# A hybrid pooling and recurrence block on one core: norm 2's reduction later, spare buffers elsewhere, and two results added in parts

## The chip, the cores and the metric

The kernel runs on 1 core of one Trainium2 chip. The metric is the device time of one execution in microseconds (us), lower is better. Time before: a median of 2389.03 us over 3 runs (2384.92 to 2390.30). The profiled execution is one more run of the same kernel; its own time was 2389.73 us, of which the profile covers a span of 2388.0 us.

The engines are TensorE (PE, matrix products; PEld is its weight loading), VectorE (DVE), ScalarE (ACT), GpSimd (POOL) and SyncE (SP). SP and POOL only issue transfers where nothing else is said. Each engine executes its instructions strictly in the order in which they stand in its program.

## The reference

One layer on 512 tokens of width 2048, with 16 learned tokens put in front:

```python
u = rmsnorm(h, norm1_g)
v_pool, v_lru, v_gelu, g_pool, g_lru = jnp.split(u @ w_in, IN_SPLITS, axis=-1)
pool_out = pool_mixer(v_pool, pool_w, pool_scale)  # 4 groups: mean of a causal window of
                                                   # 2, 4, 8, 16 tokens less the token, then a 512x512 map
xc = causal_depthwise_conv(v_lru, conv_w, conv_b)
r = sigmoid(xc @ gate_a_w + gate_a_b)              # 8 heads of 256
i = sigmoid(xc @ gate_x_w + gate_x_b)
a = exp(-8 * r * softplus(-lam))
lru = scan(h_t = a_t * h_(t-1) + sqrt(1 - a_t ** 2) * (i_t * xc_t)) * gelu(v_gelu)
merged = sigmoid(g_pool) * pool_out + sigmoid(g_lru) * lru
h = h + merged @ w_out
u2 = rmsnorm(h, norm2_g)                           # "norm 2"
h = h + square(relu(u2 @ mlp_w1)) @ mlp_w2         # 2048 -> 8192 -> 2048
out = rmsnorm(h, final_g)[:, 16:]
```

## The kernel before

**Products.** All products are in float32 precision. A weight w and an activation x are each split into a high part, which TensorE takes exactly, and the rest (whi and wlo, hi and lo), and each product is three matmuls: wh·xh, wh·xl, wl·xh (`mm3`, line 370). The big products (the two gates of the merge, the MLP up and down) are computed block by block by Strassen's method: a 2x2 block product takes seven products instead of eight, in the order x11, t1, t2, x21, t3, x22, t4, which are named after their activation operand (`strassen`, line 648). They collect in three PSUM banks A, B and C. A first takes x11; ScalarE copies it out as p1. B takes t1 (copied as q5). A goes on with t2 (copied as u2). C takes x21, A goes on with t3, B with x22, A with t4. VectorE and ScalarE put the four quadrants of the result together from banks and copies (`put("11")`, `"22"`, `"12"`, `"21"`). TensorE can only go on in a bank when the copy out of it is done: t2 waits for the copy p1, t3 for the copy u2, x22 for the copy q5, t4 for put 22.

**Weights.** Class `Weights` streams all weights in one fixed sequence. For each, a load is issued on SP (raw buffers; lines 107 and 111), VectorE forms sums of blocks where Strassen's method wants them (line 128), ScalarE makes the high part (line 137) and VectorE subtracts it to give the low part (line 138). There are 4 raw buffers, 4 pairs whi/wlo, 2 buffers of sums ("sum") and 2 that hold one block longer ("w21"). `advance()` puts the next set's work into the program at fixed points; `behind` and `hold` can order a set's sums or its copies behind a named instruction.

**Stages.** (1) The projections of the input. (2) A stretch in which the last head of the recurrence ("GA 7", gs70 and gs71 being its two blocks of 128 channels), the last pooling group ("VP 15", "PW 3") and the first gate product (`gl0`) meet. Here `evac_VP` takes channels 15 of the pooling out of PSUM (pv15), adds shifted copies of it four times on POOL (pw15, line 564; a window of 16 tokens), and forms pd15 on VectorE, whose two halves are TensorE's operand for the 48 matmuls of PW 3. ScalarE scales the results into po12 to po15 (line 586), which are stored to DRAM from SP; po buffers come in rotation, so that po14 takes one out of which an earlier store or load must have gone. `lru` runs the recurrence: two square roots (line 534, with a load of ScalarE's function table ahead of them), products, the scans on VectorE (line 545). (3) The 16 further gate products and the output projection. (4) Norm 2: its sum of squares, `ssq`, is collected on VectorE while the last part of h is formed; a matmul with a matrix of ones (`ps_r`, line 993, in `middle`) sums it over the 128 partitions, and a chain of six operations makes `rho` from it, by which the first MLP result, y0, is scaled. The first product of the MLP up runs with x11, x21 and t1 interleaved, since their last operands come late. (5) MLP up, 32 Strassen blocks. (6) MLP down: the blocks b1 to b38. The first two groups, [1, 3] and [2, 4], and [32, 38], [33, 37], [34, 36] near the end are computed in pairs by `strassen_pair` (line 725), which shares each weight between two blocks; in a pair, p1, u2 and q5 of the second block need a place of their own (`spare`): p1 and u2 lie in the tile `scale`, which is free by then, and q5 lies in the last quarter of the second block's result tile e (`es[1][:, 3 * HS :]`, HS is 256). The result e of a block up to b33 is added into h in DRAM by one accumulating transfer issued on POOL, `hsp<-e` (line 1115). e1 and e2, and e3 and e4, use the same two buffers by turns. Operands of later blocks are read from DRAM into slots (line 1028), split by ACT and DVE (lines 1044 and 1045).

The order on each engine is the program's order after a scheduler has moved instructions between the fixed points; the pieces quoted with the change are from that final order.

## Time and profile before

| | |
|---|---|
| median of 3 runs | 2389.03 us (2384.92 to 2390.30) |
| profiled execution, its own time | 2389.73 us |
| its span | 2388.0 us |
| mean granted TensorE clock | 0.994 |
| TensorE busy | 2347.3 us (98%), 40.7 us of the span without a matmul |
| weight loading (PEld) | 2300.1 us (96%) |
| VectorE | 1922.5 us (81%) |
| ScalarE | 1212.3 us (51%) |
| GpSimd | 315.5 us (13%) |
| data moved | 418.73 MB, 175 GB/s on average |

[...] A row of a timeline gives the start, the duration, the engine, the line of the kernel, the operation, out<-in with the names of the program (buffer numbers left out), partitions x elements, how many instructions the row holds, and in brackets how long the engine was idle just before and what ended that. A row of windows gives a stretch, its length, each engine's busy time in it with the number of instructions, the granted TensorE clock (1.00 is full speed), the share of the DMA engines and the GB/s they moved. Line numbers are those of the kernel before.

### The profile page before, as it was taken

What the parts mean: (1) busy time and instruction counts of PE and PEld (TensorE: products, weight loads), DVE (VectorE), ACT (ScalarE), POOL (GpSimd) and SP (SyncE); (2) the same over time, 40 slices, a digit from 0 to 9 for tenths busy, and PEclk for the clock granted to TensorE, in tenths of its full rate; (3) what the DMA queues carried; (4) which work ended last, traced back from release to release, by engine and by line L of the source; (5) the groups of instructions that cost most, each with busy time, mean ns of one, the idle gap of its engine ahead of it and who ended that gap; (6) DMA issues with size and microseconds to landing.
All of it is one profiled execution on the core that took longest, in us unless ns stands there. A gap on an engine that the chain in (4) does not pass through costs nothing. (4 is left out here: it accounts for less than half of the span.)

```text
span 2388.0 us, 46263 instructions
## 1 busy us (share of the span) xinstructions
PE 2347.3 (98%) x19254; PEld 2300.1 (96%) x19254; DVE 1922.5 (81%) x2356; ACT 1212.3 (51%) x1632; POOL 315.5 (13%) x435
## 2 busy tenths in 40 slices
PE   8999999999999999999999999999989999999997
PEld 8999999989999999888999999999989999999997
DVE  7866766588888887378989888888879888888877
ACT  6654645355555554244445444444455555555544
POOL 0224342300000001033000000000110000000013
PEclk9999999999999999999999999999999999999999
DMA  5255554654444447568544544555576666666662
GB/s 198 89 168 173 172 177 166 257 186 150 143 149 143 151 149 261 181 209 283 186 156 153 161 153 159 167 166 162 173 213 173 186 181 182 196 188 188 175 185 107
DMA packets 115858, 418.73 MB, mean 175 GB/s; under 512 B 14112, under 2 KB 18080, under 8 KB 113984
## 3 DMA queue, kind: packets, MB, share of 16 engines
q1 hardware_dynamic: 77040, 253.40, 32.9%
q0 software_dynamic: 38464, 162.29, 21.0%
q8 instruction: 150, 2.46, 0.4%
q14 instruction: 60, 0.49, 0.1%
q10 hardware_dynamic: 144, 0.10, 0.0%
HBM read 324.89 MB, written 90.31 MB: 174 GB/s over the span
## 5 line engine op out<-in xcount | busy, mean ns | idle before, releaser
L138 DVE TENSOR_TENSOR wlo<-raw,whi 128x1024 fp32r<-128x1024 f32 (+2 forms) x388 | 467.2, 1206 | 116.9 <-ACT whi L137 112.9
L137 ACT ACTIVATE whi<-raw 128x1024 fp32r<-128x1024 f32 (+2 forms) x388 | 398.9, 1034 | 318.0 <-issue 78.9
L137 ACT ACTIVATE whi<-sum 128x1024 fp32r<-128x1024 f32 (+3 forms) x267 | 279.0, 1045 | 454.2 <-DVE sum L128 234.8
L138 DVE TENSOR_TENSOR wlo<-sum,whi 128x1024 fp32r<-128x1024 f32 (+3 forms) x267 | 320.1, 1199 | 73.0 <-ACT whi L137 68.1
L370 PE MATMUL ps_A<-a,whi 128*128 128x256 f32 x2048 | 354.5, 277 | 0.0
L370 PE MATMUL ps_Ab<-a,whi 128*128 128x256 f32 x1728 | 308.8, 279 | 4.1 <-ACT u_b L746 2.1
L370 PEld LDWEIGHTS ps_A<-a,whi 128*128 128x128 f32 x2048 | 308.6, 188 | 0.7 <-issue 0.5
L370 PE MATMUL ps_A<-a,wlo 128*128 128x256 f32 x1024 | 282.9, 276 | 0.0
L370 PEld LDWEIGHTS ps_Ab<-a,whi 128*128 128x128 f32 x1728 | 263.9, 190 | 4.7 <-DVE a L1045 2.4
L370 PE MATMUL ps_Ab<-a,wlo 128*128 128x256 f32 x864 | 240.6, 279 | 0.0
L128 DVE TENSOR_TENSOR sum<-sum,raw 128x1024 f32<-128x1024 f32 (+4 forms) x178 | 213.7, 1201 | 5.5
L370 PEld LDWEIGHTS ps_A<-a,wlo 128*128 128x128 f32 x1024 | 192.3, 188 | 0.0
L370 PE MATMUL ps_B<-a,whi 128*128 128x256 f32 x1024 | 177.5, 276 | 0.0
L370 PEld LDWEIGHTS ps_Ab<-a,wlo 128*128 128x128 f32 x864 | 164.2, 190 | 0.0
L370 PE MATMUL ps_vl<-a,whi 128*128 128x272 f32 (+1 forms) x896 | 163.3, 285 | 0.0
L370 PE MATMUL ps_vp<-a,whi 128*128 128x256 f32 (+1 forms) x896 | 162.8, 284 | 0.0
L370 PE MATMUL ps_wo<-a,whi 128*128 128x512 f32 x512 | 158.0, 390 | 0.0
L370 PEld LDWEIGHTS ps_B<-a,whi 128*128 128x128 f32 x1024 | 154.2, 188 | 0.0
L370 PE MATMUL ps_Bb<-a,whi 128*128 128x256 f32 x864 | 152.5, 276 | 0.4 <-DVE a L1045 0.4
L370 PE MATMUL ps_B<-a,wlo 128*128 128x256 f32 x512 | 141.5, 276 | 0.0
L128 DVE TENSOR_TENSOR sum<-w,raw 128x1024 f32<-128x1024 f32 (+3 forms) x89 | 106.5, 1197 | 40.1 <-DMA raw<-w 39.7
L370 PEld LDWEIGHTS ps_vl<-a,whi 128*128 128x128 f32 x896 | 138.2, 189 | 0.3
(336 smaller groups left out, 5854.2 us busy)
## 6 DMA issues: line engine op xcount, KB each, us to landing
raw<-w SPq DMA_DIRECT2D x168, 512.0 KB, 4.3
raw<-w_in SPq DMA_DIRECT2D x135, 512.0 KB, 3.8
w<-w SPq DMA_DIRECT2D x56, 512.0 KB, 4.2
a<-ysp POOLq DMA_DIRECT2D x20, 896.0 KB, 6.1
hsp<-e POOLq DMA_DIRECT2D x33, 512.0 KB, 6.5
ysp<-t POOLq DMA_DIRECT2D x31, 512.0 KB, 4.9
w<-w_in SPq DMA_DIRECT2D x24, 512.0 KB, 3.9
ysp<-y POOLq DMA_DIRECT2D x31, 384.0 KB, 5.1
```

The costliest lines, as they stand in the source:

```text
L128: nc.vector.tensor_tensor(self.raw[o], self.raw[x], self.raw[y], op=ALU.add)
L137: nc.scalar.activation(hi[:, s], raw[:, s], AF.Copy)
L138: nc.vector.tensor_tensor(lo[:, s], raw[:, s], hi[:, s].bitcast(F32), op=ALU.subtract)
L370: PE.matmul(o, a, b, start=first and i == 0, stop=last and i == 2, skip_group_check=True)
```

## The change

It has seven parts.

1. In the last pooling channel (c == 15) the four window additions run on VectorE instead of POOL.
2. po14 and po15 no longer take two rotating buffers but the two halves of one buffer of the weight sums (tag "sum"). Both square roots of the last head, not only that of its first block, are now ordered behind the copy p1 of gl0.
3. `behind` holds back the sums of the sets from first_set + 6 on, no longer from + 2, until the last scan is done, and `hold` orders set first_set + 5 behind gl0's copy u2.
4. Norm 2's matmul with ones, `ps_r`, stands behind t3 and x22 of the first MLP product instead of ahead of its t2. The chain to rho and y0's scaling follow it; ssq and v2 live in a pool of their own (`rs`) until then. `finish_h` stores h by halves of the channels instead of halves of the tokens.
5. In all pairs, q5 of the second block lies in the first half of `scale` (p1's place, so it is copied after put 11) instead of the last quarter of e.
6. The quadrants lie in e in another order (n = 1 - a + 2b), so that 22's half and 12's neighbour each other; the tables of channels and weights on the host side and the output's assembly follow it.
7. For the pairs [1, 3] and [2, 4] each block's e is added into h in three transfers (512 columns after put 22, which covers 11 and 22; 256 after put 12; 256 after put 21) instead of one.

```diff
+                                    else tc.issue_after(W.u2.ins) if i == W.first_set + 5
...
                 root = S.activation(r, r, AF.Sqrt)
-                if hd == HEADS - 1 and co == 0:
-                    W.root = root
+                if hd == HEADS - 1:
+                    W.roots.append(root)
...
-                W.behind = lambda i: (tc.issue_after(scan.ins) if 1 < i - W.first_set < 21
+                W.behind = lambda i: (tc.issue_after(scan.ins) if 5 < i - W.first_set < 21
...
-                G.tensor_tensor(n[:, lo:T], s[:, lo:T], s[:, lo - win : T - win], op=ALU.add)
+                (V if c == KD - 1 else G).tensor_tensor(n[:, lo:T], s[:, lo:T], s[:, lo - win : T - win], op=ALU.add)
...
-                z = (keep if g == 3 else tmp)(f"po{c}")[:, :SEQ]
+                if c == 14:
+                    last_two = sums_pool.tile([P, SW], F32, tag="sum", name="po14", bufs=2)
+                if c < 14:
+                    z = (keep if g == 3 else tmp)(f"po{c}")[:, :SEQ]
+                else:
+                    z = last_two[:, m % 2 * SEQ : (m % 2 + 1) * SEQ]
...
                 if name == "gl0":
-                    tc.add_manual_dep(W.root.ins, done.ins.name,
+                    for root in W.roots:
+                        tc.add_manual_dep(root.ins, done.ins.name,
...
         product(B, "x22", False)
+        if norm is not None:
+            norm(done)
         put("12", B, u2)
...
-        spare = {"p1": scale[:, :HS], "u2": scale[:, HS:SEQ], "q5": es[1][:, 3 * HS :]}
+        spare = {"p1": scale[:, :HS], "u2": scale[:, HS:SEQ], "q5": scale[:, :HS]}
...
         product(C, "x21", True)
+        put("11", C, p1)
         copy(q5[1:], B[1:])
-        put("11", C, p1)
...
-            n = a + 2 * b if by_half else 2 * a + b
+            n = 1 - a + 2 * b if by_half else 2 * a + b
...
+    def norm2(done):
+        t = bank("r", "", SEQ)
+        with tc.issue_after(done.ins):
+            PE.matmul(t, ones, ssq, start=True, stop=True, skip_group_check=True)
+        a, b = ssq, v2
+        V.scalar_tensor_tensor(rho, t, EPS * D, v2, op0=ALU.add, op1=ALU.mult)
...
+        norm_stage.close()
+        scaled_later.pop()()
...
+            if (j, c) == (0, "22") and z is not None:
+                scaled_later.append(lambda: put(c, o, None))
+                return
...
+    def adding(e, p):
+        put = put_plain(e, True)
+
+        def put_and_add(c, x, z):
+            put(c, x, z)
+            at = {"22": slice(HS, 3 * HS), "12": slice(3 * HS, 4 * HS), "21": slice(0, HS)}.get(c)
+            if at:
+                nc.gpsimd.dma_start(h_sp[p][:, at], e[:, at], accum_op=ALU.add)
+        return put_and_add
...
+            puts = [adding(e, x % WIN) if n < 2 else put_plain(e, True) for e, x in zip(es, g)]
...
-        if t < JS + 2:
+        if n >= 2 and t < JS + 2:
             for x, e in zip(g, es):
                 nc.gpsimd.dma_start(h_sp[x % WIN], e, accum_op=ALU.add)
```

ScalarE where PW 3 ends and gl0 begins, from po14 to the copy u2 of gl0. In the names, `ps_pw14` is a bank of PW 3, `gs700` and `gs701` are the roots' operands (blocks 0 and 1 of the last head), the first `scale_80<-ps_Agl0` row is the copy p1, the second the copy u2, and whi83 to whi85 are the high parts of gl0's t2, x21 and a later weight set. Before:

```order
L586 ACTIVATE po14_5475<-ps_pw14_5462,par_71 128x512
L527 ACTIVATE e71_5507<-e71_5507 128x528
L137 ACTIVATE whi83_5499<-raw83_5424 128x1024
L586 ACTIVATE po15_5491<-ps_pw15_5478,par_71 128x512
L534 ACT_TABLE_LOAD
L534 ACTIVATE gs701_5374<-gs701_5374 128x528
L672 ACTIVATE scale_80<-ps_Agl0_5548 128x256
L534 ACTIVATE gs700_5359<-gs700_5359 128x528
L137 ACTIVATE whi84_5628<-w2181_5414 128x1024
L137 ACTIVATE whi85_5660<-sum80_5418 128x1024
L700 ACTIVATE scale_80<-ps_Agl0_5548 128x256
```

With the change:

```order
L594 ACTIVATE po14_5475<-ps_pw15_5478,par_71 128x512
L138 ACTIVATE whi83_5498<-raw83_5424 128x1024
L530 ACTIVATE e71_5506<-e71_5506 128x528
L138 ACTIVATE whi84_5627<-w2181_5414 128x1024
L681 ACTIVATE scale_80<-ps_Agl0_5547 128x256
L537 ACT_TABLE_LOAD
L537 ACTIVATE gs700_5359<-gs700_5359 128x528
L537 ACTIVATE gs701_5374<-gs701_5374 128x528
L710 ACTIVATE scale_80<-ps_Agl0_5547 128x256
L138 ACTIVATE whi85_5659<-sum80_5418 128x1024
```

The two roots and their table load stood ahead of the copies p1 (one of them) and u2; now both stand behind p1. whi85 stood ahead of the copy u2, and now stands behind it.

TensorE in the first MLP product, where the interleaved x11, x21 and t1 end (`ps_A0`, `ps_C0`, `ps_B0` with whi284, whi285, whi286) and t2 begins (whi287). Before:

```order
L370 MATMUL ps_A0_12353<-a2_899,wlo284_12310 128x256
L370 MATMUL ps_C0_12355<-a2_899,whi285_12340 128x256 x2
L370 MATMUL ps_C0_12355<-a2_899,wlo285_12341 128x256
L370 MATMUL ps_B0_12354<-a2_899,whi286_12349 128x256 x2
L370 MATMUL ps_B0_12354<-a2_899,wlo286_12350 128x256
L993 MATMUL ps_r_12531<-ssq2_11054,ones_72 128x512
L370 MATMUL ps_A0_12353<-a1_84,whi287_12464 128x256 x2
L370 MATMUL ps_A0_12353<-a1_84,wlo287_12465 128x256
```

With the change the same place reads on from t1 to t2, and the matmul `ps_r` stands between x22 (whi289) and t4 (whi290):

```order
L371 MATMUL ps_B0_12356<-a1_84,whi289_12503 128x256 x2
L371 MATMUL ps_B0_12356<-a1_84,wlo289_12504 128x256
L371 MATMUL ps_B0_12356<-a1_84,whi289_12503 128x256 x2
L371 MATMUL ps_B0_12356<-a1_84,wlo289_12504 128x256
L1013 MATMUL ps_r_12572<-ssq2_11056,ones_72 128x512
L371 MATMUL ps_A0_12355<-a1_84,whi290_12540 128x256 x2
L371 MATMUL ps_A0_12355<-a1_84,wlo290_12541 128x256
L371 MATMUL ps_A0_12355<-a1_84,whi290_12540 128x256 x2
```

`ps_r` was ahead of t2; now the rows of t2, t3 and x22 stand ahead of it.

ScalarE in the pair [2, 4], from the copies p1 and q5 to put 21 (`u2_b2` is u2 of block 2, the `scale_80<-ps_Ab4` row behind it u2 of block 4, `ps_Bb4` is the bank out of which q5 of block 4 is copied; a2 is the slot that is split). Before:

```order
L746 ACTIVATE q5_b2_20044<-ps_Bb2_20038 128x256
L137 ACTIVATE whi517_20066<-sum344_20025 128x768
L137 ACTIVATE whi518_20089<-raw347_19968 128x768
L137 ACTIVATE whi519_20118<-w21345_19799 128x768
L746 ACTIVATE e4_20035<-ps_Bb4_20039 128x256
L746 ACTIVATE u2_b2_20043<-ps_Ab2_20036 128x256
L746 ACTIVATE scale_80<-ps_Ab4_20037 128x256
L1044 ACTIVATE a2_899<-a2_899 128x1536
L1044 ACTIVATE a2_899<-a2_899 128x256
L137 ACTIVATE whi520_20146<-sum344_20025 128x768
L137 ACTIVATE whi521_20172<-raw346_19945 128x768
L137 ACTIVATE whi522_20200<-raw348_19989 128x640
```

With the change:

```order
L757 ACTIVATE q5_b2_20045<-ps_Bb2_20039 128x256
L138 ACTIVATE whi517_20067<-sum344_20028 128x768
L138 ACTIVATE whi518_20090<-raw347_19965 128x768
L138 ACTIVATE whi519_20119<-w21345_19796 128x768
L757 ACTIVATE u2_b2_20044<-ps_Ab2_20037 128x256
L757 ACTIVATE scale_80<-ps_Ab4_20038 128x256
L1062 ACTIVATE a2_899<-a2_899 128x1536
L1062 ACTIVATE a2_899<-a2_899 128x256
L138 ACTIVATE whi520_20147<-sum344_20028 128x768
L138 ACTIVATE whi521_20175<-raw346_19942 128x768
L138 ACTIVATE whi522_20205<-raw348_19988 128x640
L138 ACTIVATE whi523_20233<-sum348_20231 128x640
L757 ACTIVATE scale_80<-ps_Bb4_20040 128x256
```

The copy of q5 of block 4 stood ahead of both u2 copies and wrote into e4; now it stands behind them and four weight copies, and writes into `scale`.

POOL at the same two pairs, before:

```order
L1028 DMA a1_84<-ysp8_131 128x1792
L1115 DMA hsp1_116<-e1_19875 128x1024
L1115 DMA hsp3_118<-e3_19876 128x1024
L1115 DMA hsp2_117<-e2_20034 128x1024
L1115 DMA hsp4_119<-e4_20035 128x1024
L1115 DMA hsp5_120<-e5_20233 128x1024
```

With the change:

```order
L1131 DMA hsp3_118<-e3_19873 128x256
L1131 DMA hsp1_116<-e1_19872 128x256
L1131 DMA hsp3_118<-e3_19873 128x256
L1131 DMA hsp2_117<-e2_20035 128x512
L1131 DMA hsp4_119<-e4_20036 128x512
L1131 DMA hsp2_117<-e2_20035 128x256
L1131 DMA hsp4_119<-e4_20036 128x256
L1131 DMA hsp2_117<-e2_20035 128x256
L1131 DMA hsp4_119<-e4_20036 128x256
L1146 DMA hsp5_120<-e5_20238 128x1024
```

Where each block had one transfer of 1024 columns it has three, of 512, 256 and 256 (the first rows of e1 and e3 stand above these).

61 lines of the change are left out of this document (30 added, 31 removed).

## The prediction

> **What bounds the kernel now.** I read the page's busy times first, then the waits of TensorE, then windows around each place that the change touches, and last single rows of the timeline there.
>
> ```profile
> span 2388.0 us, 46263 instructions
> PE 2347.3 (98%) x19254; PEld 2300.1 (96%) x19254; DVE 1922.5 (81%) x2356; ACT 1212.3 (51%) x1632; POOL 315.5 (13%) x435
> ...
> PE ps_Ab L370 <- ACT u_b L746: 5.3, 2, 3.3
> PE ps_Ab L370 <- DVE e L783: 2.8, 1, 2.8
> PE ps_Agl L370 <- ACT scale L700: 2.5, 1, 2.5
> ...
> PE ps_r L993 <- DVE ssq L859: 1.8, 1, 1.8
> PE ps_Bgl L370 <- ACT po L586: 1.5, 1, 1.5
> PE ps_Agl L370 <- ACT scale L672: 1.3, 1, 1.3
> ```
>
> TensorE is busy for 98% of the span, and the change takes no matmul away. So only time in which TensorE stands still, or runs below full speed, can be won: 40.7 us of stalls (2388.0 less 2347.3) and the slow stretches behind some of them. The waits view (us in total, times, longest) names the targets: the copies u_b (5.3 in two places: the pair [2, 4] and a pair near the end) and put e (2.8), both in the pairs; the copies into scale and po around gl0 (2.5, 1.5, 1.3); ssq at norm 2 (1.8). That is 15.2 us, a third of it all.
>
> The second part of the price is the clock. Windows, one for each place (columns: stretch; its us; busy us and count of PE, PEld, DVE, ACT, POOL; granted clock; DMA share; GB/s):
>
> ```profile
> 464.93:477.46 12.53, 11.73 (x50) 8.94 (x49) 7.16 (x7) 9.80 (x14) 4.67 (x5) 1.00 1.04 419
> 477.46:505.78 28.32, 23.03 (x169) 22.14 (x168) 22.18 (x27) 13.21 (x18) 1.68 (x3) 0.88 0.75 262
> 494.20:500.80 6.60, 6.44 (x29) 6.14 (x30) 6.25 (x8) 2.91 (x5) 0.33 (x1) 0.51 0.93 339
> 1118.00:1150.00 32.00, 30.16 (x245) 28.97 (x244) 31.87 (x50) 16.77 (x27) 4.92 (x8) 1.00 0.71 232
> 1757.60:1768.00 10.40, 7.15 (x38) 7.08 (x38) 6.08 (x9) 5.44 (x9) 0.00 (x0) 0.67 0.22 79
> 1780.70:1788.00 7.30, 4.52 (x25) 4.42 (x25) 6.63 (x10) 1.23 (x2) 0.49 (x1) 0.77 0.17 68
> 2307.30:2314.00 6.70, 4.65 (x27) 4.60 (x27) 3.92 (x6) 2.87 (x6) 2.75 (x6) 0.75 1.02 394
> ...
> 1835.88 5.48 PE ps_Ab L370 x48
> ```
>
> The last row, from the chain of waits, is a stretch that runs undisturbed: 48 matmuls of 256 columns in 5.48 us, 0.114 each. Against it every window can be priced by its count. The clock is at 0.51, 0.67, 0.77 and 0.75 in the windows behind the waits of 2.5, 3.3, 2.8 and 2.1 (the second of the 5.3), and 1.00 around norm 2, where the wait is 1.8.
>
> **The change, stage by stage.**
>
> *Around gl0 (parts 1 to 3).* The 168 matmuls of gl0 need 168 × 0.114 = 19.2 us and took 28.32, so 9.1 us are there; PW 3 took 12.53 with 11.73 busy, another 0.8. The ceiling is 9.9. What held it:
>
> ```profile
> 459.26 0.71 DVE L558 TENSOR_TENSOR pv<-ps_vp,scale 128x528 f32<-128x528 f32 x1 [2.38 <-PE ps_vp L370]
> 465.02 1.30 POOL L564 TENSOR_TENSOR pw<-pw 128x513 f32<-128x513 f32 x1
> 466.36 0.69 DVE L567 SCALAR_TENSOR_TENSOR pd<-pw,pv 128x512 f32<-128x512 f32 x1 [6.39 <-POOL pw L564]
> 481.09 0.69 ACT L586 ACTIVATE po<-ps_pw,par 128x512 f32<-128x512 f32 x1 [2.34 <-DMA pl<-po]
> 483.86 1.28 ACT L534 ACT_TABLE_LOAD   x1
> 485.15 0.64 ACT L534 ACTIVATE gs<-gs 128x528 f32<-128x528 f32 x1
> 485.70 0.36 ACT L672 ACTIVATE scale<-ps_Agl 128x256 f32<-128x256 f32 x1
> 487.73 1.26 DVE L545 TENSOR_TENSOR_SCAN xc<-n,gs 128x528 f32<-128x528 f32 x1
> 489.50 1.22 DVE L128 TENSOR_TENSOR w<-w,raw 128x1024 f32<-128x1024 f32 x1
> 490.75 1.07 ACT L137 ACTIVATE whi<-w 128x1024 fp32r<-128x1024 f32 x1 [4.16 <-DVE w L128]
> 493.88 0.37 ACT L700 ACTIVATE scale<-ps_Agl 128x256 f32<-128x256 f32 x1
> ```
>
> VectorE waits 6.39 us for POOL's four additions. On VectorE they cost about what pv and pd do, 0.7 each: 459.97 + 4 × 0.7 = 462.8, so pd is ready near 463.5 instead of 467.05, before PW 3 starts at 464.93, and wins its 0.8. ScalarE then waited 2.34 for the transfer of an old po; a buffer of the sums is free by then, so the po copies follow the matmuls of PW 3. The table load (1.28) and a root (0.64) stood ahead of copy p1 and stand behind it now. The weight copy at 490.75 waited 4.16 for a sum that VectorE had put behind the scan, and the copy u2 (493.88) stood behind it; now that sum stands ahead of pv.
>
> The new chain, laid out with these durations: po15 at 476.8 to 477.5, the two weight copies to 479.7, p1 to 480.1, table and roots to 482.5; TensorE ends PW 3 near 476.2, x11 at 478.9, t1 at 481.6, t2 at 484.3, u2 is copied at once. ScalarE is ahead of TensorE throughout. Next to be late is VectorE: the scans move forward with the roots, to end near 487.3, and the low half of set first_set + 5, held behind u2, near 488.5, against x22's start at 489.8: 1.3 us of margin. VectorE's own new load is 2.8 us at a place where it idled 6.39. On SP, a load of weights moves ahead of stores of pooled results, and these ahead of stores of the scans; with a DMA share of 1.04 in PW 3 no queue there can be moved for free, but what reads these stores comes with the end of the gates' first blocks, 20 us on. Bounds: the whole 9.9; or half, 5, if VectorE's chain takes the place of ScalarE's, with a wait behind which the clock drops again. The margin of 1.3 is nearer the first: I take **9**.
>
> *Norm 2 (part 4).*
>
> ```profile
> 1128.43 1.23 DVE L138 TENSOR_TENSOR wlo<-sum,whi 128x1024 fp32r<-128x1024 f32 x1
> 1130.31 1.12 PE L993 MATMUL ps_r<-ssq,ones 128*128 128x512 f32 x2 [1.84 <-DVE ssq L859]
> 1133.04 1.22 DVE L138 TENSOR_TENSOR wlo<-sum,whi 128x1024 fp32r<-128x1024 f32 x1
> ```
>
> The 1.84 us on ssq go, but VectorE is busy for 31.87 of the 32 us of this window, and TensorE lives on what it makes. t2's low weights end at 1129.66; t2 (24 matmuls, 2.72) then ends near 1132.4 and x22's low weights are ready only at about 1134.0 (1134.26 before). So TensorE waits there instead, and ps_r is paid later (0.57, from its start to t2's at 1130.88, up to its 1.12). The chain to rho lies behind x22 and is needed only by y0, behind TensorE's work. Bounds: 0.7 won, if the rho chain's removal brings the low weights as much forward, or 1.5 lost, if both ps_r and a later y0 count in full. I take **0**.
>
> *The first two pairs (parts 5 to 7).*
>
> ```profile
> 1749.19 1.79 POOL L1115 DMA_DIRECT2D hsp<-e  x2 [6.77 <-ACT e L781]
> 1760.21 0.38 ACT L746 ACTIVATE e<-ps_Bb 128x256 f32<-128x256 f32 x1 [5.92 <-DMA hsp<-e]
> 1760.38 0.83 DVE L128 TENSOR_TENSOR sum<-w,raw 128x640 f32<-128x640 f32 x1 [3.51 <-DMA raw<-w]
> 1764.89 0.95 DVE L138 TENSOR_TENSOR wlo<-sum,whi 128x768 fp32r<-128x768 f32 x1
> 1770.64 0.39 ACT L781 ACTIVATE e<-ps_Ab 128x256 f32<-128x256 f32 x1 [0.97 <-PE ps_Ab L370]
> 1772.04 7.83 DMA raw<-w
> ...
> DMA to landing us min/median/max: 5.3/7.2/10.1
> ...
> DMA to landing us min/median/max: 7.2/8.6/10.1
> ```
>
> The last two lines are landing times of the accumulating transfers: of the eight between 1749 and 1841, and of the first two alone. q5 of block 4 waited 5.92 on ScalarE until e3's transfer, the second, had landed (1750.0 + 10.1 = 1760.1); the u2 copies behind it held t3. By count, 1757.6 to 1768.0 lost 10.40 − 38 × 0.114 = 6.1 us and 1780.7 to 1788.0 7.30 − 25 × 0.114 = 4.5: 10.6 in all. With q5 in scale, u2 is copied right behind t2, and t3's 18 matmuls run from 1757.6 to 1759.7. But the wait on e is not gone: put 11 of block 2 and then of block 4, on VectorE, write into the buffers that e1's and e3's transfers read, and now all three of each must have landed. Behind these puts are queued the sum of 1760.38, a slot's split and the low weights of x22 (1764.89 before). The parts are issued as the quadrants are ready, from 1746.8 on instead of 1749.19, but POOL spends about 0.9 us on each issue (1.79 for two): six take 5.1 us, the last goes out by about 1751.9, against 1750.98. The same bytes start 2.4 us earlier, so the load behind the 3.51 lands earlier as well. Laid out: low weights of x22 at 1761.5 to 1762.7 instead of 1764.89 + 0.95, a stall of some 2 us instead of 3.25, and the end of the block at 1766 to 1768 instead of 1770.64: 2.5 to 4.4 won. The load at 1772.04 took 7.83 because it ran beside the whole transfers of e2 and e4; now it goes out 3 to 4 us earlier, with half of those bytes gone before, and most of the second 4.5 is won. Bounds: 2 (the first dip stays) to 10.6 (both go). I take **7**, the middle of the first and nearly all of the second.
>
> *Near the end (part 5 alone).*
>
> ```profile
> 2308.69 0.38 ACT L746 ACTIVATE e<-ps_Bb 128x256 f32<-128x256 f32 x1 [5.74 <-DMA hsp<-e]
> 2318.74 0.63 ACT L1137 ACTIVATE a<-a 128x512 fp32r<-128x512 f32 x1 [3.73 <-DMA a<-ysp]
> ```
>
> The same q5 waited 5.74; the window lost 6.70 − 27 × 0.114 = 3.6. e's transfer is whole here as before, so only put 11 still waits until 2308.6, at VectorE. What is late next is the read of ysp that ended the wait of 3.73 at 2318.74, which does not move; up to 1 us is given back there, more if it reaches further (bound 1.5). I take **3**.
>
> The sum is 9 + 0 + 7 + 3 = 19: the profiled execution's 2389.73 becomes 2370.7. The median lies 0.70 below that execution: **2370.0**.
>
> **Rivals.**
>
> *The pairs keep their first dip* (the puts of e2 and e4 wait for the last part, issued 0.9 later than the whole one was). For it: that later issue and the median landing of 7.2. Against it: the bytes start earlier. The pairs then bring 2.5: 2374.5.
>
> *VectorE takes over around gl0*, and 5 are won of 9: 2374.0. For it: 22.18 of 28.32 us busy there. Against it: the margin of 1.3.
>
> *The clock does not depend on these stalls.* Then the slow stretches stay, losing 6.60 × 0.49 + 10.40 × 0.33 + 7.30 × 0.23 + 6.70 × 0.25 = 10.0 us, and only 9 of 19 come: 2380. Against it: each dip stands right behind a wait of about 2.0 us or more, and none behind 1.84. [...]
>
> *Slower: the parts are served one after the other, each at the price of a whole one.* At 5.3 each, six last 31.8 us, from 1746.8 to 1778.6; put 11 and what VectorE has behind it (0.83 + 2.1 + 0.42 + 0.95 = 4.3) would bring x22's low weights to 1782.9, 17 us later than before, and the second pair perhaps 8 more. Less the 12 won elsewhere: 2389.0 + 25 − 12 = 2402. It decides from about 4.2 us a part, where the pairs lose 12. Against it: a transfer's bytes are halved or quartered, and whole ones overlapped: the first two, issued 0.9 apart from 1749.2 on, landed after 7.2 and 10.1, the second 3.8 behind the first. [...]
>
> *Nothing happens*, because the load of 1760.38 or another transfer holds each place at the same time: 2389.
>
> **How the numbers follow.** Forecast 0.60; pairs keep the dip 0.15; VectorE takes over 0.12; clock 0.05; nothing 0.03; slower 0.05. The low end takes the winning bounds: 9.9 + 0.7 + 10.6 + 3.6 = 24.8, so 2364.2. The high end takes the losing ones, 5 − 1.5 + 2 + 1.5 = 7, so 2382; a little inside it, at 2381, all cases but the last two are held. A measurement of this kernel can tell about 0.2% (4.8 us) from no change; all cases but the last two win more: faster 0.92, same 0.03, slower 0.05.
>
> **What the profile after would show.** Right: pd follows pv without a wait on POOL; no waits of TensorE on po or scale around gl0, and the clock at 1.00 there; gl0's window near 20 us. At norm 2 ps_r without a wait on ssq, but a wait of the same size on a low weight or a copy. In the pairs, no ScalarE wait on hsp<-e ahead of u2; the next wait of x22 below 2.5 us. Wrong: VectorE waiting for hsp<-e at put 11 past 1762; landings of the parts above 4.2 us one after another; a dip of the clock where no stall stands; new waits in gates' first blocks for the stores of the scans.

## The result, and the profile after

The changed kernel takes 2371.59 us (median of 4 runs, 2369.89 to 2375.76) beside 2387.19 for the kernel before (median of 4 runs, 2384.92 to 2390.30): a ratio of 0.9936, with a 95% interval of 0.9918 to 0.9955, or 15.3 us less (10.7 to 19.6). A second set of runs gave 2373.46 beside 2387.19, 0.9943 (0.9926 to 0.9959). The profiled execution took 2369.89, against 2389.73 before.

The page's busy times, and TensorE's waits (us in total, times, longest), of the changed kernel:

```profile
span 2368.1 us, 46287 instructions
PE 2339.6 (99%) x19254; PEld 2293.5 (97%) x19254; DVE 1924.2 (81%) x2360; ACT 1214.2 (51%) x1632; POOL 318.5 (13%) x439
...
PE ps_v L371 <- ACT whi L138: 6.7, 1, 6.7
PE ps_Ab L371 <- DVE a L1063: 1.8, 1, 1.8
PE ps_pw L366 <- DVE v L481: 1.6, 1, 1.6
PE ps_Ab L371 <- ACT p_b L757: 1.6, 1, 1.6
...
PE ps_Ab L371 <- DVE e L794: 0.7, 1, 0.7
```

In this profile all six waits that the change aimed at are gone or under 1 us (e went from 2.8 to 0.7). New among those of over 0.5 us are 1.6 on p_b near the end and 0.6 on p at norm 2, both below, and 0.6 on gl0's put 22, ahead of its t4. (`ps_pw <- DVE v`, at 254 us, far ahead of what was changed, was 1.3 before.) The windows that answer to those of before (stretch; its us; busy us and count of PE, PEld, DVE, ACT, POOL; clock; DMA share; GB/s): gl0, the first dip in the pairs, the second, and the pair near the end.

```profile
476.80:496.60 19.80, 19.23 (x168) 19.02 (x167) 17.84 (x23) 10.66 (x15) 1.66 (x3) 1.00 0.97 363
...
1748.30:1758.70 10.40, 10.27 (x83) 9.68 (x82) 9.65 (x16) 5.39 (x9) 4.71 (x6) 1.00 0.58 132
1765.00:1775.00 10.00, 9.26 (x79) 9.04 (x79) 8.71 (x12) 4.34 (x7) 0.86 (x1) 1.00 0.50 135
2287.00:2294.00 7.00, 7.00 (x64) 7.00 (x63) 4.38 (x8) 3.84 (x5) 3.19 (x6) 1.00 1.03 368
```

gl0's 168 matmuls take 20.0 us up to the next product (28.32 before; the window leaves out the last 0.2), and the clock is at 1.00 in all four. Ahead of gl0 and in its middle the order is as laid out:

```profile
461.42 2.17 DVE L567 TENSOR_TENSOR pw<-pw 128x525 f32<-128x525 f32 x3
463.63 0.69 DVE L570 SCALAR_TENSOR_TENSOR pd<-pw,pv 128x512 f32<-128x512 f32 x1
...
477.00 0.69 ACT L594 ACTIVATE po<-ps_pw,par 128x512 f32<-128x512 f32 x1 [0.18 <-PE ps_pw L366]
480.59 0.36 ACT L681 ACTIVATE scale<-ps_Agl 128x256 f32<-128x256 f32 x1
480.97 1.28 ACT L537 ACT_TABLE_LOAD   x1
485.17 0.39 ACT L710 ACTIVATE scale<-ps_Agl 128x256 f32<-128x256 f32 x1 [1.73 <-PE ps_Agl L371]
...
488.56 1.20 DVE L139 TENSOR_TENSOR wlo<-sum,whi 128x1024 fp32r<-128x1024 f32 x1
```

pd starts at 463.63 (forecast near 463.5), the last po at 477.00 (476.8), and the held low weights at 488.56 (ready "near 488.5" was forecast; they end at 489.8, and TensorE reaches x22 at 490.4, so the margin was 0.6 and not 1.3). ScalarE now waits for TensorE at the copy u2 (485.17), not the other way round.

**Stages.** To see where the time went in every profile, I take the start of the first matmul at four pairs of marks, the same in all kernels: *gl0*, from its first matmul to the first of the next gate product (28.32 us in the first profile of before); *norm 2*, from the first MLP matmul to x21 of the fifth MLP block (88.39); *pairs*, from the first matmul of b1 to x21 of b8 (93.46); *end*, from x21 of the pair [33, 37] to x21 of b35 (38.29). The table gives the time of each profiled execution, and its differences from these in each stage, in us; the kernels are those of the next section.

| profile | its time | gl0 | norm 2 | pairs | end |
|---|---|---|---|---|---|
| before | 2389.73 | 0 | 0 | 0 | 0 |
| before, second profile (before_again) | 2386.86 | -0.83 | +2.64 | -2.69 | -2.08 |
| changed | 2369.89 | -8.31 | -0.90 | -8.17 | -2.37 |
| changed, second profile (after_again) | 2372.21 | -8.38 | -0.60 | -6.98 | -1.76 |
| gl0_alone | 2382.95 | -8.40 | +3.66 | -0.93 | -1.69 |
| norm_early | 2370.96 | -8.38 | +0.54 | -8.13 | -1.69 |
| e_whole | 2376.76 | -8.38 | +1.82 | -7.34 | -0.31 |
| q5_in_e | 2377.11 | -8.31 | +3.75 | -3.80 | -1.55 |
| adds_pool | 2376.13 | -7.33 | +0.92 | -7.33 | -0.51 |
| sums_late | 2374.48 | -3.14 | -0.38 | -7.70 | -2.16 |
| one_root | 2372.08 | -8.46 | -1.04 | -7.85 | -0.18 |
| po_rotating | 2377.56 | -1.62 | -0.24 | -8.07 | -0.09 |
| two_more | 2378.62 | -8.30 | +6.33 | -8.78 | -0.69 |
| left_out | 2367.33 | -8.37 | +0.08 | -7.53 | -4.23 |

### The profile page after: what moved, and what is told of

Its sections match the earlier page's. It is cut to its first block, busy times and chain, and to the rows that moved or that the text cites. A ratio compares the mean times of both kernels' runs of the same rounds, so it can differ in the third digit from the quotient of the medians.

```text
span 2368.1 us, 46287 instructions
## 1 busy us (share of the span) xinstructions
PE 2339.6 (99%) x19254; PEld 2293.5 (97%) x19254; DVE 1924.2 (81%) x2360; ACT 1214.2 (51%) x1632; POOL 318.5 (13%) x439
## 3 DMA queue, kind: packets, MB, share of 16 engines
q8 instruction: 150, 2.46, 0.4%
## 4 chain that ended last, share of the span: by engine, by line
PE 65%; issue 23%; DVE 4%; DMA 3%; POOL 3%; ACT 2%; POOLq 0%; ACTq 0%; DVEq 0%; SPq 0%
PE ps_Ab L371 13%; PE ps_Bb L371 7%; PE ps_vl L371 5%; PE ps_vp L371 5%; PE ps_Age L371 4%; PE ps_Agl L371 4%; PE ps_Agp L371 4%; PE ps_wo L371 3%; PE ps_Cb L371 3%; PE ps_Bge L371 2%; PE ps_Bgp L371 2%; PE ps_Bgl L371 2%; PE ps_pw L366 2%; PE ps_A L371 2%; PE ga L371 1%
## 5 line engine op out<-in xcount | busy, mean ns | idle before, releaser
L371 PEld LDWEIGHTS ps_vp<-a,whi 128*128 128x128 f32 x896 | 138.2, 188 | 0.0
```

The source lines that it names most:

```text
L371: done = PE.matmul(o, a, b, start=first and i == 0, stop=last and i == 2, skip_group_check=True)
```

## The experiments

adds_pool, sums_late, one_root, po_rotating, left_out and before_again ran once each, the others four to eight times. What an edit is worth is therefore read from the stages of the profiles, and how far a stage repeats tells what such a difference is worth: the two profiles of the changed kernel agree to 0.1 us around gl0, but differ by 1.2 in the pairs.

### Around gl0: the parts alone, and one by one

**gl0_alone.** The kernel before with the parts 1 to 3, all of them, and nothing else.

> The kernel before with the parts 1 to 3 alone (around gl0). Theory: the stages' gains are independent and add, and this one is worth 9 to 10 us: a time of about 2378 beside 2387 for the kernel before, no wait of TensorE on po or scale around gl0, full clock there, and the waits on ssq, u_b and e later on as before. Rival: a later stage that lives on transfers gives the lead back, so that less than 4 us are left at the end (2383 or more).

Measured: 2379.85 us beside 2385.95, 0.9973 (0.9962 to 0.9984), or 6.4 us less (3.8 to 9.1). The stage won 8.4, and PW 3 ahead of it another 1.3 (11.2 us instead of 12.53), together the 9 to 10 of the theory. The median lies 1.9 above the theory's 2378. The profile can explain this only in part, since the profiled execution, 2382.95, is the slowest of the eight (2377.26 to 2382.95): in it norm 2 came out 3.7 longer. So gl0's gain does not need the other parts, but part of the lead can be given back, at norm 2.

**adds_pool.** The changed kernel with

```diff
-                (V if c == KD - 1 else G).tensor_tensor(n[:, lo:T], s[:, lo:T], s[:, lo - win : T - win], op=ALU.add)
+                G.tensor_tensor(n[:, lo:T], s[:, lo:T], s[:, lo - win : T - win], op=ALU.add)
```

> The changed kernel with the four window additions of the last pooling channel back on POOL. Theory: pd is ready 3 to 4 us later, TensorE waits for the second half of PW 3 as before (0.6 and 0.2), and the lead at the end of gl0 is 0.8 to 2 us less. Rival: the later pd pushes the sums, which now stand ahead of it, and ScalarE with them: 3 us or more.

Measured: 7.3 instead of 8.3 to 8.4 won in gl0. TensorE's waits of 0.6 and 0.2 in PW 3 are back, which lies ahead of the stage and takes 12.5 us again instead of 11.2. So 2.3 us are lost in all: the theory's mechanism, at a little more than its 0.8 to 2.

**sums_late.** The changed kernel with

```diff
-                                    else tc.issue_after(W.u2.ins) if i == W.first_set + 5
...
-                W.behind = lambda i: (tc.issue_after(scan.ins) if 5 < i - W.first_set < 21
+                W.behind = lambda i: (tc.issue_after(scan.ins) if 1 < i - W.first_set < 21
```

> The changed kernel with the weight sums held behind the last scan from first_set + 2 on again, and no hold behind u2 (part 3 undone). Theory: u2 stands ahead of the late weight copy now only by the roots' move, so t3 and x21, whose weights come from these sums, wait instead: 4 to 6 us of the 8.4 are lost, with a wait of over 2 us on a low weight and a drop of the clock. Rival: the roots and po alone brought the gain: less than 1.5 us lost.

Measured: 3.1 won, so 5.2 of the 8.3 are this part's; up to 3.4 of the 5.2 are the clock, which was at half speed for 6.8 us behind the wait (an estimate, half of that time). The timeline of sums_late shows the copy of the weight waiting for its sum, and TensorE for the copy:

```profile
488.11 1.06 ACT L138 ACTIVATE whi<-w 128x1024 fp32r<-128x1024 f32 x1 [3.39 <-DVE w L129]
489.22 0.80 PE L371 MATMUL ps_Agl<-a,whi 128*128 128x256 f32 x2 [2.20 <-ACT whi L138]
```

The wait was on the high weight's copy, where "a low weight" was expected; the size held. The matmul that waits is the first of t3. So the weight w that is copied here is t3's, and in the orders quoted with the change whi84 is the weight of t3, whi83 that of x21 and whi85 that of x22.

**po_rotating.** The changed kernel with

```diff
-                if c == 14:
-                    last_two = sums_pool.tile([P, SW], F32, tag="sum", name="po14", bufs=2)
-                if c < 14:
-                    z = (keep if g == 3 else tmp)(f"po{c}")[:, :SEQ]
-                else:
-                    z = last_two[:, m % 2 * SEQ : (m % 2 + 1) * SEQ]
+                z = (keep if g == 3 else tmp)(f"po{c}")[:, :SEQ]
```

> The changed kernel with po14 and po15 in the rotating buffers again (part 2 without the roots undone). Theory: ScalarE waits for the transfer of an older po once more, 2 us or more, and all its copies behind it; TensorE waits 1 to 2.5 at t1 or t2: 1.5 to 3 us lost around gl0. Rival: the po copies come some 3 us earlier but so do the transfers that they wait for: under 1 lost.

Measured: 1.6 won, 6.7 lost: more than twice the theory, of which up to 1.7 is the clock (3.4 us at half speed). In the timeline of po_rotating, ScalarE waits twice, and the copy p1 (L676), for which TensorE stands still, comes behind these waits:

```profile
476.04 0.69 ACT L589 ACTIVATE po<-ps_pw,par 128x512 f32<-128x512 f32 x1 [4.18 <-DMA pl<-po]
482.03 0.69 ACT L589 ACTIVATE po<-ps_pw,par 128x512 f32<-128x512 f32 x1 [3.38 <-DMA pl<-po]
485.47 0.80 PE L371 MATMUL ps_Agl<-a,whi 128*128 128x256 f32 x2 [5.26 <-ACT scale L676]
```

**one_root.** The changed kernel with

```diff
-                if hd == HEADS - 1:
+                if hd == HEADS - 1 and co == 0:
                     W.roots.append(root)
```

> The changed kernel in which only the root of the last head's first block is ordered behind copy p1, as before. Theory: the table load and the other root (1.9 us) stand ahead of p1 again, TensorE waits 1 to 1.5 for it at t2, and 1 to 2 us of the 8.4 around gl0 are lost, with no drop of the clock. Rival: ScalarE is so far ahead now that p1 is in time nevertheless: under 0.5 lost.

Measured: 8.46 won, none lost: the rival held. With the po copies in time, ScalarE has the table load and a root done before TensorE needs p1 (copied at 481.08 in one_root; TensorE did not wait). So the order of the roots, to which the prediction gave a wait of 1.3, brings nothing beside the other parts. The parts' prices (1.0, 5.2, 6.7, 0) add to 12.9 for a stage worth 8.3: each late thing hides behind the others.

### Norm 2

**norm_early.** The changed kernel with `ps_r` and the chain to rho back in `middle`, ahead of t2 (part 4 undone, but for the layout in which h is stored).

```diff
      def middle():
...
+        t = bank("r", "", SEQ)
+        PE.matmul(t, ones, ssq, start=True, stop=True, skip_group_check=True)
...
-        strassen(j, X.get, put, **{0: dict(head=head, middle=middle, norm=norm2), 8: dict(between=lambda: split_slot(0)), 31: dict(hooks=last)}.get(j, {}))
+        strassen(j, X.get, put, **{0: dict(head=head, middle=middle), 8: dict(between=lambda: split_slot(0)), 31: dict(hooks=last)}.get(j, {}))
```

> The changed kernel with norm 2's matmul with ones back ahead of t2 (part 4 undone, but for the way in which h is stored). Theory: VectorE sets the pace there, so the wait of about 1.8 us on ssq comes back and the wait on a low weight goes: 0 to 1 us slower than the changed kernel, not to be told in the time, but in the trace at the end of the first MLP product. Rival: the wait on ssq makes the clock drop now, or holds all that follows: 2 us or more slower.

Measured: 2372.27 us, a ratio of 0.9943 (0.9927 to 0.9958) to before: not to be told from the changed kernel. The wait on ssq came back, at 2.5, and the stage was 1.1 to 1.4 longer than in the two profiles of the changed kernel. But e_whole, q5_in_e and adds_pool, which all have the late ps_r, took longer still there (+0.92 to +3.75). So the differences at norm 2 are not those of ps_r's place, and the next run was to tell what they are.

**after_again.** The changed kernel once more.

> The changed kernel once more, for a second profile. Theory: what norm 2 gives back (from the first MLP product to its fifth block: 0.9 us won in the first profile, but 1.8 and 3.8 lost in two kernels with the same code up to there) differs from execution to execution, because VectorE's row of work there begins with a load's landing; so this profile shows a value between 0.9 won and 3.8 lost, and the stages gl0 (8.3 to 8.4 won) and the first pairs (8.1 to 8.2) the same to 0.3. Near the end 0.3 to 2.4. Rival: the profile repeats the first to 0.5 us in each stage, and the differences belong to the kernels.

Measured: 2373.46; gl0, norm 2 and the end within 0.6 of the first profile, the pairs 1.2 longer (a wait of 1.5 on e where the first had 0.7). Norm 2 repeated, as the rival said, but the cause is not in the instructions of the stage, which are the same up to b1 in four of these profiles (changed twice, e_whole, q5_in_e: -0.90, -0.60, +1.82, +3.75). What differs is when VectorE's unbroken row of work begins, which is at the landing of one weight. The rows of the timelines in which VectorE waits for that landing:

The kernel before:

```profile
1105.85 1.23 DVE L128 TENSOR_TENSOR sum<-w,raw 128x1024 f32<-128x1024 f32 x1 [1.55 <-DMA raw<-w]
```

before_again:

```profile
1106.28 1.23 DVE L128 TENSOR_TENSOR sum<-w,raw 128x1024 f32<-128x1024 f32 x1 [3.37 <-DMA raw<-w]
```

norm_early, with the matmul that waits:

```profile
1097.01 1.23 DVE L129 TENSOR_TENSOR sum<-w,raw 128x1024 f32<-128x1024 f32 x1 [1.65 <-DMA raw<-w]
1121.45 1.12 PE L1004 MATMUL ps_r<-ssq,ones 128*128 128x512 f32 x2 [2.46 <-DVE ssq L870]
```

gl0_alone, the same two rows:

```profile
1099.10 1.23 DVE L129 TENSOR_TENSOR sum<-w,raw 128x1024 f32<-128x1024 f32 x1 [1.84 <-DMA raw<-w]
1123.56 2.07 PE L1001 MATMUL ps_r<-ssq,ones 128*128 128x512 f32 x2 [3.45 <-DVE ssq L867]
```

The changed kernel, whose ps_r is late:

```profile
1095.97 1.22 DVE L129 TENSOR_TENSOR sum<-w,raw 128x1024 f32<-128x1024 f32 x1 [1.89 <-DMA raw<-w]
```

q5_in_e, late too:

```profile
1096.90 1.23 DVE L129 TENSOR_TENSOR sum<-w,raw 128x1024 f32<-128x1024 f32 x1 [2.48 <-DMA raw<-w]
```

Measured back from the first MLP matmul of the same profile (1119.83, 1119.06, 1110.35, 1111.47, 1111.41, 1108.81), that row starts 14.0, 12.8, 13.3, 12.4, 15.4 and 11.9 us ahead. Where ps_r is early, this and the wait on ssq add up to the same number: 14.0 + 1.84, 12.8 + 3.02, 13.3 + 2.46, 12.4 + 3.45 are all 15.8 to 15.9. VectorE's row takes its fixed time, and TensorE waits for the rest. Where it is late, the loss follows the same line: leads of 16.0, 15.4, 15.1, 14.8 and 14.7 us go with differences in the table of -1.04, -0.90, -0.60, -0.24 and -0.38, leads of 13.6, 13.1 and 11.9 with +0.92, +1.82 and +3.75. Early, 14.0, 13.3, 12.8 and 12.4 go with 0, +0.54, +2.64 and +3.66. At equal lead, late against early is +0.4 at 14.0, +0.9 at 13.3, -0.3 at 12.8 and -0.7 at 12.4 (between neighbours): part 4 brings nothing that these runs can show. Part of these differences is the clock: of the profiles in the table, the five above +1 (before_again, gl0_alone, e_whole, q5_in_e, two_more) are the ones with a stretch at half speed in this stage, of 3.4 us in before_again and e_whole and of 6.8 in the others, which costs up to 1.7 and 3.4 us. Of the four waits on ssq above, the two at the shortest leads, 3.02 and 3.45, are the ones in profiles with such a stretch. What sets that landing was not settled. The load took 5.1 to 6.5 us from issue to landing, and its issue stood 18.0 to 21.4 us ahead of the first MLP matmul, so that most of the difference is already there when it is issued.

**left_out.** The changed kernel without the last four additions into ssq, and without the two reads of ysp near the end (the split there works on what the slot holds).

```diff
-        else:
+        elif p < 6:
             for a in range(2):
                 V.tensor_tensor(ssq, ssq, x[:, a], op=ALU.add)
...
-                nc.gpsimd.dma_start(yl.bitcast(F32), y_sp[m // 2][:, slice(0, SEQ) if m % 2 else slice(SEQ, 2 * SEQ)])
```

> The changed kernel without two pieces of work: the last four of the additions into ssq (2.7 us of VectorE at norm 2), and the two reads of ysp near the end (what is split there is what the slot held before). Both falsify the numbers. Theory: VectorE's row of work, which begins with a load's landing, sets the pace at norm 2, so norm 2 comes out 1.5 to 2.7 us better than the line on which the kernels lie so far (the same loss for the same lag of that landing behind TensorE); and the reads take back what part 5 brings near the end, so that the step there is 3 to 4 us won instead of 0.3 to 2.4. Rivals: norm 2 lies on the line (something else sets it); the end wins under 2.4, as before, since the slot's readers or a weight hold ScalarE there as well.

Measured, at norm 2: +0.08 at a lead of 13.5, where the line of late kernels has about +1.1 and adds_pool, at 13.6, +0.92 (neither with a slow clock). So about 1 of the 2.7 us of VectorE's work came back in this one profile: the direction of the theory, at under the expected 1.5. Near the end: 4.2 won, a little more than the theory's 3 to 4 (below).

### The first two pairs

**e_whole.** The changed kernel with one transfer for each e, issued when e is complete:

```diff
-            puts = [adding(e, x % WIN) if n < 2 else put_plain(e, True) for e, x in zip(es, g)]
+            puts = [put_plain(e, True) for e, x in zip(es, g)]
...
-        if n >= 2 and t < JS + 2:
+        if t < JS + 2:
```

> The changed kernel with one whole transfer for each of e1, e2, e3 and e4 (part 7 undone, q5 still in scale). Theory: the early parts matter as much as q5's place, since put 11 of block 4 on VectorE waits for e3's transfer, and the sum, the split and the low weights of x22 behind it: TensorE stands 3 to 4 us at x22 instead of t3, the clock drops, 4 to 8 us slower than the changed kernel. Rival: q5's place alone did it: u_b no longer waits, and the time is within 2 us of the changed kernel.

Measured: 2376.76 us, 0.9966 (0.9952 to 0.9979). Its median is 5.2 above the changed kernel's, inside the theory's 4 to 8, but the mechanism of the theory did not appear in the profile (2376.76, the median itself): 7.3 won in the pairs, against 7.0 to 8.8 in the kernels with the parts. Most of the rest lies at norm 2 (2.7 behind the changed kernel's first profile) and near the end (2.1), where it has the changed kernel's code, and some 1.3 outside the four stages. For the pairs the rival held; that the seven runs as a whole are slower is not explained by the edit, and stays open. The timeline of e_whole shows that put 11 did not wait for any transfer, and the load behind it for 1.57 only:

```profile
1751.50 0.42 DVE L790 TENSOR_TENSOR e<-ps_Cb,p_b 128x256 f32<-128x256 f32 x1
1753.49 0.83 DVE L129 TENSOR_TENSOR sum<-w,raw 128x640 f32<-128x640 f32 x1 [1.57 <-DMA raw<-w]
1754.23 2.09 DVE L1063 TENSOR_TENSOR a<-a 128x1536 fp32r<-128x1536 f32 x2
1756.23 0.42 DVE L790 TENSOR_TENSOR e<-ps_Cb,scale 128x256 f32<-128x256 f32 x1
```

**q5_in_e.** The changed kernel with q5 of the second block in e, three transfers kept:

```diff
-    def strassen_pair(names, jobs, puts, between):
+    def strassen_pair(names, jobs, puts, between, qe):
...
-        spare = {"p1": scale[:, :HS], "u2": scale[:, HS:SEQ], "q5": scale[:, :HS]}
+        spare = {"p1": scale[:, :HS], "u2": scale[:, HS:SEQ], "q5": qe}
...
+        copy(q5[1:], B[1:])
         put("11", C, p1)
-        copy(q5[1:], B[1:])
...
-            strassen_pair([f"b{x}" for x in g], [of_slots(x) for x in g], puts, lambda: split_slot(n + 3))
+            strassen_pair([f"b{x}" for x in g], [of_slots(x) for x in g], puts, lambda: split_slot(n + 3), es[1][:, 3 * HS :])
```

> The changed kernel with q5 of the second block back in the last quarter of e, in all pairs (part 5 undone, three transfers kept). Theory: with the parts issued early, the last part of e3 lands near the time at which u_b is due, so that the first two pairs lose 0 to 1.5 us, and the pair near the end, whose transfer is whole, loses its 2.4 again: 2 to 4 us slower than the changed kernel. Rival: q5's place is the cause of the gain in the first pairs too: ScalarE waits 3 us or more on a part of e3, the clock drops, 8 to 11 us slower.

Measured: 2376.87 us, 0.9962 (0.9947 to 0.9977), 5.3 above the changed kernel; 3.8 won in the pairs instead of 7 to 8. Neither number held: in the pairs more than the theory's 0 to 1.5 is lost, in the time more than its 2 to 4 and less than the rival's 8 to 11. The kind of loss is the rival's: ScalarE waits for the last part, and the u2 copies behind it.

```profile
1752.56 0.39 ACT L757 ACTIVATE e<-ps_Bb 128x256 f32<-128x256 f32 x1 [4.46 <-DMA hsp<-e]
1753.27 0.50 PE L371 MATMUL ps_Ab<-slot,whi 128*128 128x256 f32 x2 [1.90 <-ACT u_b L757]
```

**before_again.** The kernel before once more.

> The kernel before once more, for a second profile to measure the stages against. Theory: its landing at norm 2 lags otherwise than in the first profile and its wait on ssq with it, by the same amount; near the end it is 1.5 to 1.7 us faster than the first profile, like both kernels with the old place of q5 there, so that part 5 is worth nothing there in the end; around gl0 and in the first pairs it repeats to 0.3. Rival: near the end it repeats the first profile, and the 1.7 of those two kernels comes from their lead.

Measured: 2386.86 us. gl0 was 0.8 shorter than in the first profile and norm 2 longer by 2.6, with the wait on ssq at 3.0; near the end it was 2.1 shorter, somewhat more than the theory's 1.5 to 1.7. Around gl0 and in the pairs it did not repeat to 0.3: the pairs were 2.7 us shorter, with the same late q5. Its waits of TensorE there were 1.5 (3.3 in the first profile) and 2.5 (2.8), and the clock stayed at 1.00 behind both. Against the mean of the three profiles with the old pairs (0, -2.69, -0.93, so -1.2), the change is worth 6.6 there on average (nine profiles with both parts, -7.8), the q5 move alone 6.1 (e_whole), the three transfers alone 2.6 (q5_in_e).

### Near the end, and a try at more

**two_more.** The changed kernel with the last four additions into ssq on POOL, and the first of the two reads of ysp issued on SP.

```diff
-                V.tensor_tensor(ssq, ssq, x[:, a], op=ALU.add)
+                (G if p > 5 else V).tensor_tensor(ssq, ssq, x[:, a], op=ALU.add)
...
-                nc.gpsimd.dma_start(yl.bitcast(F32), y_sp[m // 2][:, slice(0, SEQ) if m % 2 else slice(SEQ, 2 * SEQ)])
+                (nc.gpsimd if i else nc.sync).dma_start(yl.bitcast(F32), y_sp[m // 2][:, slice(0, SEQ) if m % 2 else slice(SEQ, 2 * SEQ)])
```

> The changed kernel with two more moves: the last four additions into ssq run on POOL instead of VectorE, and the first of the two reads of ysp near the end is issued on SP instead of behind the reads of acc on POOL. Theory: VectorE's work of about 0.7 us each sets the pace at norm 2, and the read of ysp is what takes back the lead near the end (1.6 us of wait on p_b); so norm 2 comes out 2 to 3 us better than in the kernels with the same code, and the end 1.5 to 2; 2367 to 2369 beside 2371.6. Rival: another transfer or the loads of weights hold both places, and it is the same within 1.5 us.

Measured: 2378.62 us, 0.9963 (0.9950 to 0.9976), some 5 to 7 above the changed kernel: both the theory and the rival were off. Norm 2 came out 6.3 longer, of which up to 3.4 is the clock (6.8 us at half speed). POOL took 1.29 us for each of the first two additions, and 6.05 and 2.15 for the last two, of the same form (together 8.28; why was not settled), and VectorE waited 1.43 for the first pair. On SP the first read went out at 2301.66, later than the second on POOL (2298.36; what held it there was not settled), and TensorE's wait on p_b grew to 2.7. The two rows of POOL in two_more:

```profile
1104.89 2.65 POOL L872 TENSOR_TENSOR ssq<-ssq,hs 128x512 f32<-128x512 f32 x2 [0.27 <-ACT hs L867]
1117.15 8.28 POOL L872 TENSOR_TENSOR ssq<-ssq,sq 128x512 f32<-128x512 f32 x2
```

The reads matter all the same. In the changed kernel's timeline the first of them lands so late that ScalarE waits 7.59 us, and p_b, which TensorE needs for t2 of the next pair, stands behind it:

```profile
2301.15 0.63 ACT L1168 ACTIVATE a<-a 128x512 fp32r<-128x512 f32 x1 [7.59 <-DMA a<-ysp]
2304.64 0.38 ACT L757 ACTIVATE p_b<-ps_Ab 128x256 f32<-128x256 f32 x1
2305.07 0.50 PE L371 MATMUL ps_Ab<-a,whi 128*128 128x256 f32 x2 [1.57 <-ACT p_b L757]
```

Without the reads (left_out) the end won 4.2 us instead of 0.1 to 2.4, and its profile has no wait of TensorE there at all. An earlier place for these reads was not tried.

## Why the prediction was right, point by point

Forecast 2370.0, in a range of 2364 to 2381; measured 2371.59 and 2373.46. The profiled execution fell by 19.8 us, where the sum said 19, but the medians lie 15.6 apart: the sum was made on an execution of the kernel before that was among its slower ones. "The median lies 0.70 below that execution" was the smallest of the steps and one that failed: with more runs the median of before is 2387.19, 2.5 below. So the win was 3.4 us smaller than the forecast 19, and the time came out within 1.6 us of the forecast because the median of before, from three runs, had been 1.8 too high: that part is luck.

- *Around gl0, 9.* Right in size: 8.3 in gl0 against the first profile, 7.5 against the second, and another 1.3 in PW 3, which has no waits any more (the sum had 0.8 there). Its second half, VectorE's chain, did not take over; the margin was 0.6 us. The division into causes was off in one point: the table load and root ahead of p1 cost nothing once the po copies are in time.
- *Norm 2, 0.* Right, and for the reason given: VectorE sets the pace. The step that named low weights and the copy as the next to be late was right too (0.6 on p, 0.2 on a low weight). Not foreseen was that TensorE's lead arrives at a load's landing that does not move as reliably, so that up to 3.8 us of what gl0 wins is lost there in some executions, up to 3.4 of it, by estimate, by the clock behind the longer waits (6.8 us at half speed in q5_in_e).
- *The first pairs, 7.* Right in size (7.0 to 8.2 against the first profile, 6.6 against the mean of three). Wrong in its parts: the wait of put 11 until "all three of each must have landed" exists, but it cost TensorE little. In the first profile of the changed kernel and in e_whole put 11 does not wait for a transfer. In five profiles (after_again, adds_pool, sums_late, po_rotating, q5_in_e) VectorE waited 1.4 to 1.6 us at put 11 of block 2 for one of the three. In after_again:

```profile
1749.62 0.42 DVE L790 TENSOR_TENSOR e<-ps_Cb,p_b 128x256 f32<-128x256 f32 x1 [1.38 <-DMA hsp<-e]
1753.14 0.38 ACT L757 ACTIVATE scale<-ps_Bb 128x256 f32<-128x256 f32 x1 [0.77 <-DVE e L790]
```

The second row is the copy of q5 of block 4, for which x22 waits behind the puts. The forecast stall "of some 2 us" at x22 came to 0.9 at most, in e_whole as well (0.84, without that wait). q5's place is most of the gain; the three transfers add about 0.5, less than these runs tell apart.
- *Near the end, 3.* The step that failed. Against the first profile it was 0.1 to 2.4 in eight profiles with the new place of q5 and the reads as they were, but the profiles with the old place (before_again, gl0_alone, q5_in_e) have 1.5 to 2.1 as well. Compared with the clock alike, the new place is worth 0.2 to 0.3: without a drop -1.7, -1.8, -2.2 and -2.4 against -1.6, -1.7 and -2.1; with one, -0.1 to -0.5 against 0. The term "up to 1 us is given back" was mis-sized: the reads of ysp take back all of it.
- *The clock.* "Each dip stands right behind a wait of about 2.0 us or more, and none behind 1.84" was a rule from one execution, and wrong. In 14 profiles the same wait at the start of b1, 1.7 to 1.8 us long, halved the clock behind it in five and not in nine. The changed kernel and one_root, each the stall and 3 us behind it:

```profile
1728.04 0.38 PE L371 MATMUL ps_Ab<-a,whi 128*128 128x256 f32 x1 [1.77 <-DVE a L1063]
...
1728.00:1731.00 3.00, 2.96 (x15) 2.77 (x15) 3.00 (x5) 1.93 (x6) 0.00 (x0) 0.61 1.03 422
```

```profile
1727.65 0.39 PE L371 MATMUL ps_Ab<-a,whi 128*128 128x256 f32 x1 [1.78 <-DVE a L1063]
...
1727.70:1730.70 3.00, 2.31 (x15) 1.87 (x16) 3.00 (x5) 1.88 (x5) 0.00 (x0) 1.00 1.03 423
```

So the 10 us of slow clock in the first profile were partly chance: before_again had no dip in the pairs or at the end, and was 2.7 and 2.1 us shorter there. Up to the drop at the program's end the clock was at half speed for 20.5 us in the first profile of before, for 6.8 in the second, and for 3.4 in each of the two of the changed kernel. Half of such a time is lost, by an estimate from the granted 0.50: 8.5 of the 19.8 us between the first two profiles, and 1.7 of the 14.7 between the other two. That the profiled execution fell by as much as the sum said is therefore in good part luck. The rival that the clock does not depend on the stalls is refuted all the same, since gl0 ran at 1.00 in every kernel without the stalls, and in none of the four profiles with one of 2.2 us or more. What goes with a drop and what does not is told in the last section.

- *The slower rival.* The parts were not served one after the other: 12 of them landed 5.3 to 7.8 us after their issue, while POOL issued six in 5.3. The row of POOL, and the landing times in the view of the transfers' line:

```profile
1738.72 5.33 POOL L1131 DMA_DIRECT2D hsp<-e  x6 [4.93 <-DVE e L794]
...
DMA to landing us min/median/max: 5.3/6.5/7.8
```

A quarter of the bytes did not land sooner here than a whole e: the eight parts of 256 columns landed 6.1 to 7.8 us after their issue, the four of 512 columns 5.3 to 7.0, and a whole e took 5.3 to 10.1 before. But the parts overlap: the six of the pair [1, 3], issued from 1738.72 to 1742.01, landed between 1744.07 and 1749.06.

## What to carry to other kernels

Take a slow-clock stretch behind a stall of 1.7 to 2.8 us as a chance of about one half (17 of 35 here), not as a loss that is sure to come back, and make the sum against more than one profile. A wait that is removed is worth what the next late thing allows: leaving that next thing out for one run (here two reads of 256 KB) shows it in one profile. Where several late things stand behind one another, undoing them one at a time gives prices that add to more than the whole.

## What the runs showed of the hardware that was not expected

**The granted clock.** Over the 14 profiles I took every stall of TensorE of at least 1.4 us behind the start-up, and the granted clock in the 3 us behind it. Of 18 below 1.72 none was followed by a lower clock; of 25 from 1.73 to 2.05, 12; of ten from 2.1 to 2.8, five; of five from 3.0 up, all. Between 1.73 and 2.8 the length does not decide it: sums_late's 2.20 was followed by a drop and norm_early's 2.46 was not. Four more drops (two in e_whole, one each in adds_pool and two_more) stand behind shorter stalls alone, of 1.2 us at most.

The clock records of the traces show what goes with it. Up to the drop at the program's end every slow stretch is at 0.50, lasts 3.41 us or twice that, and all those of one profile begin on one grid of 3.413 us: in the first profile of before at 493.79, 1760.14, 1784.03 and 2309.68, which lie 371, 7 and 154 steps of it apart (1815.89 us in 532 steps). The two profiles of the changed kernel have their grids at different places (their stretches begin at 1728.68 and 1727.85). Here are three stretches along the grid of the changed kernel, and then two along that of one_root, around the same stall of 1.77 and 1.78 us at the start of b1:

```profile
1725.27:1728.68 3.41, 1.37 (x9) 0.89 (x8) 3.12 (x5) 3.18 (x6) 0.00 (x0) 1.00 1.02 415
1728.68:1732.09 3.41, 3.41 (x17) 3.30 (x17) 3.41 (x6) 2.21 (x5) 0.12 (x1) 0.50 0.97 395
1732.09:1735.51 3.42, 3.42 (x32) 3.42 (x32) 3.04 (x6) 3.07 (x6) 1.49 (x3) 1.00 0.71 204
```

```profile
1722.73:1726.14 3.41, 2.72 (x22) 2.32 (x20) 0.97 (x1) 2.31 (x3) 0.00 (x0) 1.00 1.01 415
1726.14:1729.56 3.42, 1.86 (x13) 1.62 (x13) 3.42 (x5) 2.97 (x5) 0.00 (x0) 1.00 1.02 415
```

In the changed kernel the stall falls into one stretch, which has no matmul for 2.04 of its 3.41 us, and the next stretch is slow. In one_root a border of the grid divides it: 0.69 and 1.56 us without a matmul, and the clock stays. Counted over the 14 profiles, from the first matmul to the last and at full clock, 23 stretches of the grid have no matmul for 1.73 us or more, about half of their length, and behind every one of them the clock is halved. Of the other 9592, which have 1.71 us or less, three are followed by a slow stretch (1.63 and 1.14 us in e_whole, 1.06 in adds_pool; why is open). So up to the last matmul a stretch of the grid without a matmul for about half of its length was enough in all 23 cases. Behind the last matmul it was not: in the first profile of before the stretch from 2374.54 has none for 1.93 of its 3.41 us, and the next one, which has none at all, is still at 1.00; 0.50 begins behind that, at 2381.36.

**Profiles of the same instructions.** Up to b1 four profiles ran the same instructions (e_whole, q5_in_e and the changed kernel twice) and reached it 5.9, 7.3, 9.3 and 9.3 us ahead of the first profile of before. The two of one and the same kernel agree; whether the other two differ by the execution or by something that goes with their programs was not settled. A difference of under 4 us between two single profiles, whatever the median says, has to be looked for in a stage before it is put down to an edit.
